# Retention operands issued behind bank copies, alternating token halves in three channel tiles, and the last token tile's residual added inside its PSUM bank

## The chip, the core and the metric

The kernel runs on one core of one Trainium2 chip. Its time is the device time of one execution in microseconds (us). A core has four engines that matter here, each with its own program that it works through in order: TensorE (PE) multiplies, with its weight loads as a second stream (PEld); VectorE (DVE) and ScalarE (ACT) do elementwise work; SyncE (SP) issues transfers (DMA) between memory and the on-chip buffer, and ACT can issue some too. Engines wait for each other by semaphores. Products of TensorE land in PSUM, which has eight banks of 512 fp32 columns on 128 partitions, and DVE or ACT read them from there.

## The reference

The kernel computes one layer on 512 tokens of width 1024, with 16 learned meta tokens put in front:

```python
u = rms_norm(x) @ w_in                 # eight groups: rnn values and gates, q, k, v, retention gates, two mixing gates
rnn: causal conv of 4 taps, sigmoid gates a and x, a linear scan over the tokens, GELU gate
ret: 4 heads, chunked retention with decay, head_rms, then * silu(gate)
mix = sigmoid(..) * (rnn @ w_branch_rnn) + sigmoid(..) * (ret @ w_branch_ret)
h = x + mix @ w_out
f = rms_norm(h) @ w_up                 # 6144 columns, causal conv of 3 taps, gelu(half) * other half
out = rms_norm(h + f @ w_down) * norm_final_g
```

Input and output are fp32.

## The kernel before

**fp32 as two fp16 parts.** Each operand is split into a high fp16 part and a low one. `split` (L92 to L96) is one ACT copy that writes the high part (L94) and one DVE SCALAR_TENSOR_TENSOR that writes the remainder (L95). A product is then three matmuls, high by high, high by low and low by high, in the order of `SPLIT = ((0,0),(0,1),(1,0))`, where the first index is that of the weights. A weight is loaded by a DMA into a tile `raw` (three buffers) and split into a tile `wt`. Of the trace's names, `xh` and `xl` are the two parts of the normalised input, `xs` those of an intermediate.

**Start.** The first ten channel tiles of `w_in` are the values of the recurrent branch (loop at L686, `n` from 0 to 9). `conv_product(n)` (L632) multiplies 1024 input rows by 128 channels for all tokens, which stand in two halves `HR` of 266 and 265 columns, each in a PSUM bank of its own. The tiles 0 to 2 were begun earlier with one half each (`early`), and do the other half here. The tiles from 3 on go through `project` (L428): all 24 matmuls of one half, then the 24 of the other. A weight tile covers half of the 1024 rows, so a channel reads two of them. Between two channels stand the 12 gate matmuls of the channel three before (`rnn_gates`, L654, on `xs` and `gw`). `conv_taps` (L642) reads the product from PSUM, once on ACT (L644) and three times on DVE (L646), and only then is its pair of banks free; there are four pairs, shared with the gates, so that a channel's product waits for the taps of the channel two before it.

**Mixing.** After retention, the kernel runs the gates and the two branches' products. `fast_products` (L872) is a form of Strassen's algorithm with seven products, which share the banks `pa`, `pb` and `pe`. Where a bank is used on by the next product, its content is first put aside by an ACT copy, `keep` (L887), into `kept` or `last`; this copy has high priority and is remembered in `last_keep[0]`. The product T1, for one, can't start in `pa` until `kept` is copied from it. The gated retention outputs `or` are turned into operands `ob` of such a product by `ob_forms`: `differences` (four DVE operations, L1082 to L1085), `plain` and `formed` (five splits, each on ACT and on DVE). They stand in the list `pending`, and `flush` (L1108) takes one of them at each step of the mixing (`advance`). The order of each engine's program follows from a scheduler that looks at priorities and at what an instruction has been told to stand behind (`tc.issue_after`). `behind_copy()` tells it to stand behind the last bank copy, but only while `gating[0]` is true; at L1161 that is set to False, and so `flush` in the mixing puts its step in without any such rule.

**End.** The output is made for four token tiles of 128 rows. `down_plain` (L1602) multiplies the last weight unit into a bank, 12 matmuls of 512 columns. Then, per token tile in the order 2, 3, 0, 1: DVE adds the residual (`hu`, L1702), ACT squares and sums (L1704, with its ACTIVATION_READ_ACCUMULATOR), DVE multiplies by the final weight (L1705), ACT takes the root (L1707), DVE the reciprocal (L1709), and then DVE scales 512 of the columns (L1710) and ACT the other 512 (L1712); two transfers of 128 rows by 2 KB write them out (L1711 on SP, L1713 on SP too, or, for the last tile, on ACT's queue). The last token tile is tile 1, in the bank P7. The first half of each row was multiplied by the final weight earlier (`weigh`, L1673).

Of the kernel before, what the change touches and what calls it, by code (L numbers as in the profile page):

```python
# [8 lines left out]
F32 = mybir.dt.float32  # L9
F16 = mybir.dt.float16  # L10
AF = mybir.ActivationFunctionType
ORDERED = {mybir.EngineType.PE, mybir.EngineType.Activation, mybir.EngineType.DVE}
ALU = mybir.AluOpType

P = 128
# [4 lines left out]
KD = D // P  # L20
# [33 lines left out]
def hybrid_block_kernel(ctx, tc, x, meta, norm_mix_g, w_in, conv_w, conv_b, rg_a_w, rg_a_b,  # L54
                        rg_x_w, rg_x_b, lam, w_brnn, w_bret, w_out, norm_ffn_g, w_up,
                        fconv_w, fconv_b, w_down, norm_final_g, rope_t, decay_t, out):
    nc = tc.nc
# [5 lines left out]
    work = ctx.enter_context(tc.tile_pool(name="work", bufs=8))  # L63
    small = ctx.enter_context(tc.tile_pool(name="small", bufs=4))
# [11 lines left out]
    def acc(name):  # L76
        return psum["acc"].tile([P, 2, 512], F32, name=name, tag="acc")
# [6 lines left out]
    def xslot(shape, dtype, name):  # L84
        return xp.tile(shape, dtype, name=name, tag="x")

    def piece(shape, dtype, name):
        return pieces.tile(shape, dtype, name=name, tag="s")
# [20 lines left out]
    def kmaj(w, k0, nk, c0, ncol):  # L109
        return w[k0 * P:(k0 + nk) * P, c0:c0 + ncol].rearrange("(k p) c -> p k c", p=P)  # L110
# [3 lines left out]
    def unit(nk, ncol, parts, fast=False):  # L114
        units.append((nk, ncol, parts, fast))
        return len(units) - 1
# [3 lines left out]
    for i in range(5):  # L120
        u = unit(8, 256, [(0, 0, kmaj(w_in, 0, 8, o_ur + 256 * i, 256))])
# [71 lines left out]
    def unit_load(cuts=1):  # L193

        nk, ncol, parts, fast = units[len(loaded)]
        raw = wraw.tile([P, 2048], F32, name="raw")
        n = nk * ncol
        rv = raw[:, :n].rearrange("p (k c) -> p k c", k=nk)
        for k0, c0, ap in parts:
            load(rv[:, k0:k0 + ap.shape[1], c0:c0 + ap.shape[2]], ap)  # L200
        loaded.append(len(loaded))
        if fast:
            return fast_steps(rv, nk // 2, ncol // 2)
        hk = nk // 2
        hn = hk * ncol
        tiles = []

        def step(i, c):
            def run():
                if c == 0:  # L210
                    tiles.append(wsp.tile([P, 2, 1024], F16, name="wt"))
                sl = slice(c * hn // cuts, (c + 1) * hn // cuts)
                split(tiles[i][:, 0, sl], tiles[i][:, 1, sl], raw[:, i * hn:(i + 1) * hn][:, sl], SW)
            return run

        wviews.append(lambda a, k, c0, m: tiles[k // hk][:, a, k % hk * ncol + c0:k % hk * ncol + c0 + m])
        return [step(i, c) for i in range(2) for c in range(cuts)]
# [66 lines left out]
    last_keep = [None]  # L284
    gating = [True]

    def behind_copy():

        return tc.issue_after(last_keep[0]) if gating[0] and last_keep[0] else nullcontext()
# [8 lines left out]
    def emit_step():  # L298
        u, run = steps[done[0]]
        while len(loaded) < min(u + 3, len(units)):  # L300
            queue(unit_load())
        run()
        done[0] += 1

    def queue(new):
        steps.extend((len(loaded) - 1, run) for run in new)

    def get(u):
        current[0] = max(current[0], u)
        while len(loaded) <= u:  # L310
            queue(unit_load())
        while done[0] < len(steps) and steps[done[0]][0] <= u:
            emit_step()
        return wviews[u]
# [96 lines left out]
    SPLIT = ((0, 0), (0, 1), (1, 0))  # L411

    def x_of(hi, lo):
        tv = (hi, lo)
        return lambda a, k, c0, n: tv[a][:, k, c0:c0 + n]

    xf = x_of(xh, xl)

    def half_of(ps, halves, hf):
        c0, n = (512 - halves[0][1], halves[0][1]) if hf == 0 else (0, halves[1][1])  # L420
        return ps[:, hf, c0:c0 + n]
# [3 lines left out]
        n = n or halves[0][1] + halves[1][1]  # L425
        return ps.rearrange("p a b -> p (a b)")[:, c0:c0 + n]

    def project(ps, w, col, src, halves, nk):  # L428

        for hf, (c0, n) in enumerate(halves):  # L430
            for k in range(nk):
                for aw, ax in SPLIT:
                    nc.tensor.matmul(half_of(ps, halves, hf), w(aw, k, col, P), src(ax, k, c0, n),  # L433
                                     start=k == 0 and (aw, ax) == (0, 0), stop=k == nk - 1 and aw == 1)

# [2 lines left out]
    HR = [(0, 266), (266, 265)]  # L438
# [4 lines left out]
    def project_half(ps, w, col, src, halves, hf):  # L443
        c0, n = halves[hf]
        for k in range(KD):
            for aw, ax in SPLIT:
                mm = nc.tensor.matmul(half_of(ps, halves, hf), w(aw, k, col, P), src(ax, k, c0, n),  # L447
                                      start=k == 0 and (aw, ax) == (0, 0), stop=k == KD - 1 and aw == 1)
        return mm.ins
# [182 lines left out]
    def conv_product(n):  # L632
        u, col = u_ur[n]
        if n in early:
            ps = early.pop(n)
            project_half(ps, get(u), col, xf, HR, 1)
        else:
            ps = acc("ps")
            project(ps, get(u), col, xf, HR, KD)
        return ps  # L640

    def conv_taps(n, ps):  # L642
# [43 lines left out]
    for n in range(NR):  # L686
        ps = conv_product(n)
# [41 lines left out]
    for n in range(NR):  # L729
        ps = acc("ps")  # L730
        u, col = u_ug[n // 2], (n % 2) * P
# [45 lines left out]
    for h in range(HEADS):  # L777
        t = [[piece([P, 2, T], F16, f"qk{h}{i}{m}") for m in range(2)] for i in range(2)]
# [329 lines left out]
    def flush(n=1):  # L1108

        for _ in range(min(n, len(pending))):  # L1110
            with behind_copy():
                pending.pop(0)()

    def advance(run, *names):
# [83 lines left out]
    def branch(us, src, nk):  # L1198
        ps = acc("pm")
        project(ps, get(us.pop(0)), 0, src, HH, nk)  # L1200
        tick(2)
        return run_of(ps, HH)
# [20 lines left out]
    for i in range(2):  # L1223
# [5 lines left out]
        ps = branch(u_ba, oa_of, NR)  # L1229
# [6 lines left out]
        gate_a(i + 1, after)  # L1236
    mix_first(5, branch(u_ba, oa_of, NR))
    flush(len(pending))

    def gate_b(i):  # L1240
# [23 lines left out]
    h2 = [h2p[i // 2][:, i % 2] for i in range(4)]  # L1264
# [137 lines left out]
    halves = slice(0, 256), slice(256, 512)  # L1402
# [181 lines left out]
    gfin = xslot([P, D], F32, "gfin")  # L1584
# [3 lines left out]
    o2 = out.rearrange("o t d -> (o t) d")  # L1588
    inv_d = 1.0 / D
    un = 1.0 / (SW * S_ACT)  # L1590
    sums = small.tile([P, 4, 4], F32, name="sums", bufs=1)
# [7 lines left out]
                                 start=q % 6 == 0 and tt == 0 and i == 0 and (ax, aw) == (0, 0),  # L1599
                                 stop=q % 6 == last and i == 1 and ax == 1, skip_group_check=True)  # L1600

    def down_plain(pc, tt):  # L1602

        w = wviews[u_dn[11]]
        n = 0
        for half in range(2):
            for b in range(2):
                t, c0 = acts[10 + b]["A%d%d" % (tt // 2 + 1, half + 1)]
                for ax, aw in SPLIT:
                    nc.tensor.matmul(pc, t[:, ax, c0 + tt % 2 * P:c0 + tt % 2 * P + P], w(aw, 2 * half + b, 0, 512),  # L1610
                                     start=n == 0, stop=n == 11)
                    n += 1

    def square(tt, cols, n):
# [42 lines left out]
    pd = products()  # L1657
# [9 lines left out]
    for tt in range(4):  # L1667
        junk = work.tile([P, 512], F32, name="junk", tag="w")
        nc.scalar.activation(junk.rearrange("p (a b) -> p a b", a=2),
                             h2[tt].rearrange("p (a b) -> p a b", a=2)[:, :, 0:256],  # L1670
                             AF.Square, accum_out=sums[:, tt, 0:1])

    def weigh(tt, c0):  # L1673
        v = h2[tt].rearrange("p (a b) -> p a b", a=2)[:, :, c0:c0 + 256]
        nc.vector.tensor_tensor(v, v, gfin.rearrange("p (a b) -> p a b", a=2)[:, :, c0:c0 + 256], op=ALU.mult)

    for tt in range(4):
        weigh(tt, 0)
        nc.vector.tensor_scalar(sums[:, tt, 1:2], sums[:, tt, 0:1], inv_d, EPS, op0=ALU.mult, op1=ALU.add)


    pd = products()
# [10 lines left out]
                next(run)  # L1693
    nc.scalar.activation(sq_t, sums[:, 3, 1:2], AF.Sqrt)
    for nm, tt in (("spare", 2), ("P1", 3), ("P6", 0), ("P7", 1)):
        down_plain(pd[nm], tt)
        pv = pd[nm].rearrange("p (a b) -> p a b", a=2)
        hv = h2[tt].rearrange("p (a b) -> p a b", a=2)[:, :, 256:512]
        gv = gfin.rearrange("p (a b) -> p a b", a=2)[:, :, 256:512]
        hu = work.tile([P, 512], F32, name="hu", tag="w")  # L1700
        huv = hu.rearrange("p (a b) -> p a b", a=2)
        nc.vector.scalar_tensor_tensor(huv, pv, un, hv, op0=ALU.mult, op1=ALU.add)  # L1702
        junk = work.tile([P, 512], F32, name="junk", tag="w")
        nc.scalar.activation(junk, hu, AF.Square, accum_out=sums[:, tt, 2:3])  # L1704
        nc.vector.tensor_tensor(hv, huv, gv, op=ALU.mult)  # L1705
        sd = small.tile([P, 1], F32, name="sd")
        nc.scalar.activation(sd, sums[:, tt, 2:3], AF.Sqrt, scale=inv_d, bias=sums[:, tt, 1:2])  # L1707
        rs = small.tile([P, 1], F32, name="rs")
        nc.vector.reciprocal(rs, sd)  # L1709
        nc.vector.tensor_scalar_mul(h2[tt][:, 0:512], h2[tt][:, 0:512], rs)  # L1710
        nc.sync.dma_start(o2[tt * P:(tt + 1) * P, 0:512], h2[tt][:, 0:512])  # L1711
        nc.scalar.activation(h2[tt][:, 512:1024], h2[tt][:, 512:1024], AF.Copy, scale=rs)  # L1712
        (nc.scalar if tt == 1 else nc.sync).dma_start(o2[tt * P:(tt + 1) * P, 512:1024], h2[tt][:, 512:1024])  # L1713
    psum["scope"].close()


# [45 lines left out]
```

## Time and profile before

| what | value |
|---|---|
| time, median of 3 runs | 1061.51 us (1061.37 to 1062.74) |
| profiled execution, its own time | 1061.5 us |
| span of that execution in the profile | 1059.8 us, so 1.7 us lie outside |
| granted TensorE clock | 0.999 of full speed |
| TensorE busy | 1039.7 us, 98% of the span |
| VectorE busy | 872.8 us, 82% |
| ScalarE busy | 594.0 us, 56% |

A row of the profile's timeline has the start in us from the start of the span, the duration in us, the engine, the line of the kernel, the operation, and what is written from what. `x12` stands for twelve like instructions drawn together, whose duration runs from the first's start to the last's end. The brackets at the end, such as `[0.83 <-DVE wt L95]`, give the time that the engine stood idle ahead of this row and what released it. Matmuls are pipelined: one of 266 columns is on record for 0.28 us, while the next one starts some 0.11 us after it. On DVE and ACT too, a row is some 0.1 us longer than the distance to the next one's start, where the next is ready.

### The profile page before, as it was taken

The numbers are of one execution on the slowest core, as the hardware profiler recorded it, in microseconds if no ns is written. First come the engines' busy times: TensorE is split into PE (matmuls) and PEld (weight loads), VectorE is DVE, ScalarE is ACT, GpSimd is POOL, SyncE is SP. The second block draws the span as 40 slices with busy tenths as digits, with TensorE's granted clock in tenths as the row PEclk, the third lists the DMA queues.
The fourth block names the chain that finished last, engine by engine and source line by source line (L and its number), as shares of the span: only waits on it lengthen the run. The fifth ranks groups of instructions, "written<-read, shape, count | busy, mean of one in ns | idle before, by whom it ended". The sixth has DMA issues, their size and how long they took to land.

```text
span 1059.8 us, 21437 instructions
## 1 busy us (share of the span) xinstructions
PE 1039.7 (98%) x9187; PEld 865.9 (82%) x9187; DVE 872.8 (82%) x1328; ACT 594.0 (56%) x941; POOL 6.9 (1%) x20
## 2 busy tenths in 40 slices
PE   9999999999999999999999999999999999999997
PEld 6888887875588888888888886588888888888885
DVE  6885699988669999996787885479989898988975
ACT  7568973434356768665454453375555455554442
POOL 2000000000000000000000000000000000000000
PEclk9999999999999999999999999999999999999999
DMA  9231243431012132344334356032423324214312
GB/s 295 97 127 58 81 140 120 159 123 40 1 41 93 68 105 66 107 114 128 108 113 129 98 219 194 1 116 85 160 87 113 120 81 136 65 61 139 101 41 80
DMA packets 109056, 111.52 MB, mean 105 GB/s; under 512 B 5675, under 2 KB 100625, under 8 KB 108961
## 3 DMA queue, kind: packets, MB, share of 16 engines
q1 hardware_dynamic: 108512, 109.74, 32.5%
q8 instruction: 72, 1.18, 0.5%
q10 hardware_dynamic: 160, 0.27, 0.1%
q0 software_dynamic: 288, 0.14, 0.1%
q14 instruction: 24, 0.19, 0.1%
HBM read 108.04 MB, written 2.10 MB: 104 GB/s over the span
## 4 chain that ended last, share of the span: by engine, by line
PE 72%; DVE 16%; ACT 9%; issue 2%; DMA 0%; ACTq 0%; DVEq 0%
PE ps L433 25%; PE P L1598 10%; PE pa L881 9%; DVE wt L95 5%; PE ps L1315 4%; PE pe L881 4%; PE pm L433 4%; PE ps L945 4%; ACT wt L94 2%; PE pb L881 2%; PE pa L1485 2%; PE ps L1035 2%; PE ps L447 2%; DVE rnn L680 1%; PE pa L969 1%
## 5 line engine op out<-in xcount | busy, mean ns | idle before, releaser
L433 PEld LDWEIGHTS <-wt 128*128 128x128 f16 x3840 | 372.5, 97 | 56.0 <-DVE t L770 2.6
L95 DVE SCALAR_TENSOR_TENSOR wt<-raw,wt 128x1024 f16<-128x1024 f32 (+2 forms) x286 | 310.0, 1100 | 57.1 <-ACT wt L94 56.2
L94 ACT ACTIVATE wt<-raw 128x1024 f16<-128x1024 f32 (+2 forms) x286 | 268.2, 958 | 118.7 <-PE P L1598 25.6
L881 PEld LDWEIGHTS <-wt 128*128 128x128 f16 x2016 | 195.2, 97 | 33.5 <-issue 6.7
L433 PE MATMUL ps<-x2h,wt 128*128 128x258 f16 (+1 forms) x1184 | 196.2, 272 | 0.0
L433 PE MATMUL ps<-xh,wt 128*128 128x258 f16 (+4 forms) x1056 | 179.0, 274 | 3.7 <-DVE t L770 2.9
L433 PE MATMUL ps<-x2l,wt 128*128 128x256 f16 (+1 forms) x592 | 160.9, 272 | 0.0
L433 PE MATMUL ps<-xl,wt 128*128 128x256 f16 (+4 forms) x528 | 144.5, 274 | 0.0
L1598 PE MATMUL P<-wt,act 128*128 128x256 f16 x792 | 88.3, 273 | 0.0
L1598 PEld LDWEIGHTS <-act 128*128 128x128 f16 x792 | 77.5, 98 | 9.0
L881 PE MATMUL pa<-xs,wt 128*128 128x258 f16 x576 | 71.3, 273 | 3.0 <-ACT kept L887 2.6
L1463 DVE SCALAR_TENSOR_TENSOR cv<-ps,vt,cv 128x512 f32<-128x512 f32 x80 | 59.3, 745 | 9.1 <-ACT cv L1461 8.5
L433 PE MATMUL pm<-oa,wt 128*128 128x256 f16 (+1 forms) x480 | 54.1, 273 | 0.0
L262 DVE TENSOR_TENSOR raw<-raw 128x1024 f32<-128x1024 f32 x43 | 52.4, 1219 | 0.7
L881 PE MATMUL pa<-ob,wt 128*128 128x257 f16 x384 | 45.7, 274 | 0.6 <-ACT last L887 0.5
L1315 PE MATMUL ps<-wt,mx 128*128 128x512 f16 x192 | 44.3, 378 | 0.0
L945 PE MATMUL ps<-wt,xh 128*128 128x512 f16 x128 | 38.3, 379 | 0.6 <-ACT qk L94 0.5
L1461 ACT ACTIVATE cv<-ps,vt,vt 128x512 f32<-128x512 f32 x40 | 30.5, 766 | 11.9 <-PE ps L433 11.9
L1485 PEld LDWEIGHTS <-wt 128*128 128x128 f16 x336 | 32.6, 97 | 4.4
L94 ACT ACTIVATE qk<-t 128x514 f16<-128x514 f32 (+1 forms) x16 | 10.2, 638 | 40.9 <-DVE t L772 40.9
L1315 PEld LDWEIGHTS <-mx 128*128 128x128 f16 x192 | 17.6, 98 | 18.5
L447 PEld LDWEIGHTS <-wt 128*128 128x128 f16 x288 | 27.9, 97 | 5.0 <-issue 0.6
(319 smaller groups left out, 1503.3 us busy)
## 6 DMA issues: line engine op xcount, KB each, us to landing
raw<-in_w_in SPq DMA_DIRECT2D x36, 1024.0 KB, 5.0
raw<-in_w_up SPq DMA_DIRECT2D x24, 1024.0 KB, 5.2
raw<-in_w_down SPq DMA_DIRECT2D x48, 256.0 KB, 3.4
raw<-in_w_branch_ret SPq DMA_DIRECT2D x16, 512.0 KB, 4.8
raw<-in_w_in SPq DMA_DIRECT2D x12, 512.0 KB, 4.6
raw<-in_w_branch_rnn SPq DMA_DIRECT2D x8, 640.0 KB, 4.7
raw<-in_w_out SPq DMA_DIRECT2D x4, 1024.0 KB, 5.0
xin<-in_x SPq DMA_DIRECT2D x4, 512.0 KB, 5.6
```

The lines of the kernel that those rows point to most:

```text
L94: a = nc.scalar.activation(hi, src, AF.Copy, scale=s)
L95: b = nc.vector.scalar_tensor_tensor(lo, src, s, hi, op0=ALU.mult, op1=ALU.subtract)
L262: nc.vector.tensor_tensor(pair, pair, rv[:, :, right].rearrange("p (h k) c -> p h k c", h=2), op=ALU.add)
L433: nc.tensor.matmul(half_of(ps, halves, hf), w(aw, k, col, P), src(ax, k, c0, n), start=k == 0 and (aw, ax) == (0, 0), stop=k == nk - 1 and ...
L447: mm = nc.tensor.matmul(half_of(ps, halves, hf), w(aw, k, col, P), src(ax, k, c0, n), start=k == 0 and (aw, ax) == (0, 0), stop=k == KD - ...
L881: nc.tensor.matmul(ps[:, :n], ws[k // 4](wf, aw, k % 4), src(xf_, ax, k), start=first and k == 0 and (aw, ax) == (0, 0), stop=k == last_k ...
L945: nc.tensor.matmul(pb, xf(ax, k, XF + j0, nb), w(aw, k % 4, 0, 512), start=i == 0, stop=i == 23)
L1315: nc.tensor.matmul(ps[:, n], mx[k][:, a, c0:c0 + P], wo[k // 2](aw, k % 2, n * 512, 512), start=k == 0 and (a, aw) == (0, 0), stop=k == ks ...
L1461: nc.scalar.activation(vv_, taps[2], AF.Identity, scale=vt2[:, 96 + ch:97 + ch], bias=bias)
L1463: nc.vector.scalar_tensor_tensor(vv_, taps[j], vt2[:, 48 * j + ch:48 * j + ch + 1], vv_, op0=ALU.mult, op1=ALU.add)
L1485: nc.tensor.matmul(ps[:, :258], w(wf, aw, k), x2_form(xf_, ax, k), start=first and k == 0 and (aw, ax) == (0, 0), stop=k == 3 and aw == 1, ...
L1598: nc.tensor.matmul(pd[:, 256 * tt:256 * tt + 256], t[:, ax, c0 + tt * P:c0 + tt * P + P], w(wf, aw, i), start=q % 6 == 0 and tt == 0 and i ...
```

## The change

There are three edits. First, `flush` puts each pending step behind the last bank copy in all cases, not only while `gating[0]` is true. Second, `project` gets a flag `turns`: with it the loop over the halves is the innermost, so that successive matmuls go to the two banks in turn; `conv_product` sets it for n < 6, which, as the tiles 0 to 2 take the other branch, is for the tiles 3, 4 and 5. Third, for the last token tile (`LAST = 1`) an ACT copy puts the residual, divided by the scale of the products, into the bank P7 ahead of the matmuls, and these add to it. ACT then squares straight from the bank, with the scale in its operand and an epsilon term scaled in advance (`sums[:, LAST, 3]`, a new small DVE operation), and one DVE SCALAR_TENSOR_TENSOR makes the output's half out of the bank, the reciprocal and the final weight. The two transfers each carry 256 runs of 1 KB in place of 128 of 2 KB. `weigh` becomes a SCALAR_TENSOR_TENSOR of the same size. Lines behind `project` stand one later in the changed kernel, those of the end more.

```diff
-    def project(ps, w, col, src, halves, nk):
+    def project(ps, w, col, src, halves, nk, turns=False):
-        for hf, (c0, n) in enumerate(halves):
-            for k in range(nk):
-                for aw, ax in SPLIT:
+        both = [0, 1]
+        for hfs in [both] if turns else [[0], [1]]:
+            for k, (aw, ax), hf in [(k, s, hf) for k in range(nk) for s in SPLIT for hf in hfs]:
+                    c0, n = halves[hf]
                     nc.tensor.matmul(half_of(ps, halves, hf), w(aw, k, col, P), src(ax, k, c0, n),
...
-            project(ps, get(u), col, xf, HR, KD)
+            project(ps, get(u), col, xf, HR, KD, n < 6)
...
         for _ in range(min(n, len(pending))):
-            with behind_copy():
+            with tc.issue_after(last_keep[0]):
                 pending.pop(0)()
...
+    nc.vector.tensor_scalar_mul(sums[:, LAST, 3:4], sums[:, LAST, 1:2], 1.0 / (un * un))
...
+        if tt == LAST:
+            nc.scalar.activation(pv, hv, AF.Copy, scale=1.0 / un)
+            down_plain(pd[nm], tt, True)
+            junk = work.tile([P, 512], F32, name="junk", tag="w")
+            nc.scalar.activation(junk, pd[nm], AF.Square, scale=un, accum_out=sums[:, tt, 2:3])
+            nc.scalar.activation(sd, sums[:, tt, 2:3], AF.Sqrt, scale=inv_d / (un * un), bias=sums[:, tt, 3:4])
+            nc.vector.reciprocal(rs, sd)
+            ob_ = o2[tt * P:(tt + 1) * P].rearrange("t (a b) -> t a b", a=2)
+            nc.vector.scalar_tensor_tensor(hv, pv, rs, gv, op0=ALU.mult, op1=ALU.mult)
+            nc.sync.dma_start(ob_[:, :, 256:512], hv)
+            nc.scalar.activation(hb[:, :, 0:256], hb[:, :, 0:256], AF.Copy, scale=rs)
+            nc.scalar.dma_start(ob_[:, :, 0:256], hb[:, :, 0:256])
+            break
```

TensorE, the product of a channel tile that goes through `project` (tile 4): the name `ps` is its pair of banks, and the number of columns tells the half, 266 for the first and 265 for the second. Before:

```order
L433 MATMUL ps<-xh,wt 128x266
L433 LDWEIGHTS wt
L433 MATMUL ps<-xl,wt 128x266
L433 LDWEIGHTS wt
L433 MATMUL ps<-xh,wt 128x266
L433 LDWEIGHTS wt
L433 MATMUL ps<-xh,wt 128x266
```

After:

```order
L434 MATMUL ps<-xh,wt 128x266
L434 LDWEIGHTS wt
L434 MATMUL ps<-xh,wt 128x265
L434 LDWEIGHTS wt
L434 MATMUL ps<-xl,wt 128x266
L434 LDWEIGHTS wt
L434 MATMUL ps<-xl,wt 128x265
```

The same 48 matmuls and weight loads are there, but the second half now goes along with the first, so that each part of the weights is asked for at half the pace.

ScalarE in the mixing, around 452 to 461 us of the span: `g` are the gates, `kept` is the bank copy on which T1 waits, `ob` the retention operands. Before:

```order
L920 ACT_TABLE_LOAD
L920 ACTIVATE g_5557<-g_5557 128x257
L887 ACTIVATE kept<-pa 128x257
L920 ACTIVATE g_5557<-pa 128x257
L94 ACTIVATE wt<-raw 128x1024
L920 ACTIVATE g_5556<-g_5556 128x514
L94 ACTIVATE ob_5835<-or_5016 128x257
L887 ACTIVATE kept<-pa 128x257
L94 ACTIVATE ob<-or_5017 128x514
```

After:

```order
L888 ACTIVATE kept<-pa 128x257
L921 ACT_TABLE_LOAD
L921 ACTIVATE g_5557<-g_5557 128x257
L921 ACTIVATE g_5557<-pa 128x257
L94 ACTIVATE wt<-raw 128x1024
L921 ACTIVATE g_5556<-g_5556 128x514
L888 ACTIVATE kept<-pa 128x257
L94 ACTIVATE ob_5835<-or_5016 128x257
L94 ACTIVATE ob<-or_5017 128x514
```

The second copy `kept` now stands ahead of the operand `ob_5835`, and directly behind the gate `g_5556`; the first one stands ahead of the gate's table load.

VectorE at the same place, 450 to 455 us: the sum `g_5557<-pe,last` (L908 before, L909 after) is the one that frees the bank `pe` for the product T4. Before:

```order
L95 SCALAR_TENSOR_TENSOR wt<-raw,wt 128x1024 x2
L95 SCALAR_TENSOR_TENSOR wt<-raw,wt 128x640 x2
L1206 SCALAR_TENSOR_TENSOR m<-pm,g_5346 128x514
L95 SCALAR_TENSOR_TENSOR ob<-or_4354,ob 128x514
L904 TENSOR_TENSOR g_5556<-pb,kept 128x257
L95 SCALAR_TENSOR_TENSOR ob<-y,ob 128x514
L95 SCALAR_TENSOR_TENSOR ob<-d,ob 128x514
L908 TENSOR_TENSOR g_5557<-pe,last 128x257
L95 SCALAR_TENSOR_TENSOR wt<-raw,wt 128x512
```

After:

```order
L95 SCALAR_TENSOR_TENSOR ob_5440<-or_4353,ob_5440 128x257
L95 SCALAR_TENSOR_TENSOR wt<-raw,wt 128x1024 x2
L95 SCALAR_TENSOR_TENSOR wt<-raw,wt 128x640
L1207 SCALAR_TENSOR_TENSOR m<-pm,g_5346 128x514
L95 SCALAR_TENSOR_TENSOR wt<-raw,wt 128x640
L905 TENSOR_TENSOR g_5556<-pb,kept 128x257
L95 SCALAR_TENSOR_TENSOR ob<-or_4354,ob 128x514
L95 SCALAR_TENSOR_TENSOR wt<-raw,wt 128x512
L1124 TENSOR_TENSOR or_5018<-or_5018,rt 128x514
L909 TENSOR_TENSOR g_5557<-pe,last 128x257
L95 SCALAR_TENSOR_TENSOR ob<-y,ob 128x514
L95 SCALAR_TENSOR_TENSOR ob<-d,ob 128x514
```

The two operands `ob<-y` and `ob<-d` now stand behind that sum; a weight part of 512 columns, the scaling `or_5018` (L1123 before) and the 257-column part of `ob_5440` have come ahead of it.

More of the change, by code (lines that the diff above doesn't have):

```diff
@@ L1600, in down_product, with down_plain @@
                                  stop=q % 6 == last and i == 1 and ax == 1, skip_group_check=True)
-    def down_plain(pc, tt):
+    def down_plain(pc, tt, seeded):
         w = wviews[u_dn[11]]
@@ L1610, in down_plain @@
                     nc.tensor.matmul(pc, t[:, ax, c0 + tt % 2 * P:c0 + tt % 2 * P + P], w(aw, 2 * half + b, 0, 512),
-                                     start=n == 0, stop=n == 11)
+                                     start=n == 0 and not seeded, stop=n == 11, skip_group_check=seeded)
                     n += 1
@@ L1671, in hybrid_block_kernel @@
                              AF.Square, accum_out=sums[:, tt, 0:1])
+    LAST = 1
     def weigh(tt, c0):
         v = h2[tt].rearrange("p (a b) -> p a b", a=2)[:, :, c0:c0 + 256]
-        nc.vector.tensor_tensor(v, v, gfin.rearrange("p (a b) -> p a b", a=2)[:, :, c0:c0 + 256], op=ALU.mult)
+        nc.vector.scalar_tensor_tensor(v, v, 1.0 / un if tt == LAST else 1.0,
+                                       gfin.rearrange("p (a b) -> p a b", a=2)[:, :, c0:c0 + 256],
+                                       op0=ALU.mult, op1=ALU.mult)
     for tt in range(4):
@@ L1695, in hybrid_block_kernel @@
     for nm, tt in (("spare", 2), ("P1", 3), ("P6", 0), ("P7", 1)):
-        down_plain(pd[nm], tt)
         pv = pd[nm].rearrange("p (a b) -> p a b", a=2)
-        hv = h2[tt].rearrange("p (a b) -> p a b", a=2)[:, :, 256:512]
-        gv = gfin.rearrange("p (a b) -> p a b", a=2)[:, :, 256:512]
+        hb = h2[tt].rearrange("p (a b) -> p a b", a=2)
+        hv, gv = hb[:, :, 256:512], gfin.rearrange("p (a b) -> p a b", a=2)[:, :, 256:512]
+        sd = small.tile([P, 1], F32, name="sd")
+        rs = small.tile([P, 1], F32, name="rs")
+        if tt == LAST:
[11 more added lines that the diff above has]
+            break
+        down_plain(pd[nm], tt, False)
         hu = work.tile([P, 512], F32, name="hu", tag="w")
@@ L1705, in hybrid_block_kernel @@
         nc.vector.tensor_tensor(hv, huv, gv, op=ALU.mult)
-        sd = small.tile([P, 1], F32, name="sd")
         nc.scalar.activation(sd, sums[:, tt, 2:3], AF.Sqrt, scale=inv_d, bias=sums[:, tt, 1:2])
-        rs = small.tile([P, 1], F32, name="rs")
         nc.vector.reciprocal(rs, sd)
@@ L1712, in hybrid_block_kernel @@
         nc.scalar.activation(h2[tt][:, 512:1024], h2[tt][:, 512:1024], AF.Copy, scale=rs)
-        (nc.scalar if tt == 1 else nc.sync).dma_start(o2[tt * P:(tt + 1) * P, 512:1024], h2[tt][:, 512:1024])
+        nc.sync.dma_start(o2[tt * P:(tt + 1) * P, 512:1024], h2[tt][:, 512:1024])
     psum["scope"].close()
```

## The prediction

> **What bounds the kernel now.** I read the page first: busy times and the chain that ended last.
>
> ```profile
> span 1059.8 us, 21437 instructions
> PE 1039.7 (98%) x9187; PEld 865.9 (82%) x9187; DVE 872.8 (82%) x1328; ACT 594.0 (56%) x941; POOL 6.9 (1%) x20
> PE 72%; DVE 16%; ACT 9%; issue 2%; DMA 0%; ACTq 0%; DVEq 0%
> ```
>
> TensorE is busy for 98% and makes 72% of the chain. None of the edits takes a matmul away, so the only thing to win is TensorE's idle time, 1059.8 − 1039.7 = 20.1 us of the span, and the work behind its last matmul. I therefore went through TensorE's timeline for the rows with a wait in brackets, then through ACT's and DVE's rows just ahead of each of them. The edits touch idle time at three places.
>
> **Part 1, alternating halves.** TensorE's rows at the start, first tile 4 and the gates behind it, then the first matmul of tile 5, then tile 9, which doesn't stall:
>
> ```profile
> 39.90 0.28 PE L433 MATMUL ps<-xh,wt 128*128 128x266 f16 x1
> ...
> 42.65 0.40 PE L433 MATMUL ps<-xh,wt 128*128 128x266 f16 x2 [0.83 <-DVE wt L95]
> ...
> 46.53 0.84 PE L433 MATMUL ps<-xs,gw 128*128 128x264 f16 x6
> ...
> 47.88 0.28 PE L433 MATMUL ps<-xh,wt 128*128 128x266 f16 x1
> ...
> 75.14 0.28 PE L433 MATMUL ps<-xh,wt 128*128 128x266 f16 x1
> ...
> 80.60 1.51 PE L433 MATMUL ps<-xs,gw 128*128 128x264 f16 x12
> ```
>
> and DVE's rows there, the low parts of tile 4's two weight tiles and the taps of tile 3:
>
> ```profile
> 39.00 1.22 DVE L95 SCALAR_TENSOR_TENSOR wt<-raw,wt 128x1024 f16<-128x1024 f32 x1
> ...
> 41.37 1.22 DVE L95 SCALAR_TENSOR_TENSOR wt<-raw,wt 128x1024 f16<-128x1024 f32 x1
> ...
> 44.03 2.37 DVE L646 SCALAR_TENSOR_TENSOR rnn<-ps,cwr,rnn 128x528 f32<-128x528 f32 x3
> ```
>
> Without a stall the 48 matmuls of a channel take 80.60 − 75.14 = 5.46 us, 0.114 each. Tile 4 took 46.53 − 39.90 = 6.63: it lost 1.17, as its weights' low parts were ready only at 40.22 and 42.59. With the halves in turn the first low part is wanted by the fifth matmul, at 39.90 + 4 × 0.114 = 40.36, and the second by the 29th, at 43.09. Both are there by then, so tile 4 ends at 45.36, **1.17 earlier**. Neither ACT nor DVE waits for TensorE here, so the splits don't move. What is late next is the pair of banks. Tile 5 waits for taps that end at 44.03 + 2.37 = 46.40 and would arrive at 47.88 − 1.17 = 46.71, with 0.31 to spare; the tiles behind it stand to their taps in the same way, each a little tighter or looser. Tiles 3 and 5 have no stall, and for them the order costs nothing, if changing the bank is free (a rival below).
>
> Does the gain reach the end? ACT's first wait for TensorE after that, a later wait of ACT for a transfer, and TensorE's wait at 162.75:
>
> ```profile
> 81.48 0.70 ACT L662 ACTIVATE rnn<-ps,vt 128x528 f32<-128x528 f32 x1 [1.51 <-PE ps L433]
> ```
>
> ```profile
> 153.20 2.00 ACT L94 ACTIVATE wt<-raw 128x1024 f16<-128x1024 f32 x2 [5.48 <-DMA raw<-in_w_in]
> ```
>
> ```profile
> 162.75 0.28 PE L433 MATMUL ps<-xh,wt 128*128 128x256 f16 x1 [2.30 <-DVE t L770]
> ```
>
> At 81.48 ACT waits for TensorE and had been free since 79.97, so the chain of the recurrent branch, which DVE and ACT carry from there to 162.75, starts 1.17 earlier (with 1.51 of room). The transfer awaited at 153.20 is issued when an earlier `raw` is free, that is by the same chain, so I let it move along. Bounds of the term: 0, if banks or transfers hold it, and −1.17; I take **−1.17**, as each of these waits has room in its row.
>
> **Part 2, operands behind the bank copies.** The stalls of TensorE at the beginning of the mixing:
>
> ```profile
> 425.06 1.48 PE L881 MATMUL pa<-xs,wt 128*128 128x258 f16 x12 [0.28 <-ACT kept L887]
> ...
> 439.61 1.48 PE L881 MATMUL pa<-xs,wt 128*128 128x258 f16 x12 [0.33 <-ACT kept L887]
> ```
>
> ```profile
> 453.66 0.27 PE L881 MATMUL pe<-xh,wt 128*128 128x258 f16 x1 [0.70 <-DVE g L908]
> ...
> 458.84 0.27 PE L881 MATMUL pb<-xh,wt 128*128 128x258 f16 x1
> 460.53 1.48 PE L881 MATMUL pa<-xs,wt 128*128 128x258 f16 x12 [1.42 <-ACT kept L887]
> ```
>
> ACT and DVE there:
>
> ```profile
> 438.65 0.63 ACT L920 ACTIVATE g<-g 128x514 f32<-128x514 f32 x1 [1.84 <-DVE g L915]
> ```
>
> ```profile
> 457.47 0.62 ACT L920 ACTIVATE g<-g 128x514 f32<-128x514 f32 x1
> 459.79 0.42 ACT L94 ACTIVATE ob<-or 128x257 f16<-128x257 f32 x1 [1.70 <-DVE or L1067]
> 460.11 0.37 ACT L887 ACTIVATE kept<-pa 128x257 f32<-128x257 f32 x1
> ```
>
> ```profile
> 452.59 0.68 DVE L95 SCALAR_TENSOR_TENSOR ob<-d,ob 128x514 f16<-128x514 f32 x1
> 453.19 0.41 DVE L908 TENSOR_TENSOR g<-pe,last 128x257 f32<-128x257 f32 x1
> 453.53 1.81 DVE L95 SCALAR_TENSOR_TENSOR wt<-raw,wt 128x512 f16<-128x512 f32 x2
> ...
> 457.00 0.41 DVE L915 TENSOR_TENSOR g<-pe,kept 128x257 f32<-128x257 f32 x1
> ```
>
> At 425.06 the copy comes free of the forms ahead of it and up to 0.28 goes. But at 439.61 the copy stands behind the gate of 438.65, which waits for a DVE sum that the edit doesn't move; TensorE, early, waits there for the longer, and what was won is given back: 0 for these two together.
>
> At 453.66 it gets worse. Ahead of the sum L908 there go two forms of 514 columns (0.60 each to the next start), and there come a weight part of 512 (0.60), a scaling of 514 (0.60) and a form of 257 (0.34): + 1.54 − 1.20 = +0.34, and T4 starts at 454.00.
>
> At 460.53 it gets better. In the trace, `kept` stands behind the form of 459.79, which waited 1.70 for DVE's `or`. In the new order it stands right behind the gate of 457.47. That gate waits for L915, at 457.00 before; it now has the 0.34, and two forms (1.20) ahead of it, less the weight part of 512 that has gone ahead (0.60): 457.94, so the gate is at 457.94 + 0.47 = 458.41, the copy, 0.52 behind it, at 458.93 and done at 459.30, and T1 starts at 459.35. TensorE itself comes from the product before at 458.84 + 0.11 + 0.34 = 459.29. So T1 starts 460.53 − 459.35 = 1.18 earlier, the 0.34 included. The form that had held the copy now waits alone; TensorE doesn't need it for long. Further on, ACT waits for TensorE:
>
> ```profile
> 480.22 0.74 ACT L94 ACTIVATE wt<-raw 128x640 f16<-128x640 f32 x1 [4.12 <-PE pm L433]
> ```
>
> There the engines take their time from TensorE again, and the gain stays. The new orders differ no more after about 500 us, so I leave later stalls as they are. Bounds: −2.73, if all four stalls went (0.28 + 0.33 + 0.70 + 1.42), and +0.34, if only the loss came true. I take **−1.18**, my count through the queues.
>
> **Part 3, the end.** The last matmuls, then DVE, ACT, and the transfers' issues:
>
> ```profile
> 1052.05 1.46 PE L1610 MATMUL P<-wt,act 128*128 128x512 f16 x6
> ```
>
> ```profile
> 1053.67 0.68 DVE L1702 SCALAR_TENSOR_TENSOR hu<-P,h 128x512 f32<-128x512 f32 x1
> ...
> 1055.67 0.49 DVE L1710 TENSOR_SCALAR h<-h,rs 128x512 f32<-128x512 f32 x1
> ```
>
> ```profile
> 1047.80 0.63 ACT L1704 ACTIVATE junk<-hu 128x512 f32<-128x512 f32 x1 [11.90 <-DVE hu L1702]
> ...
> 1053.27 0.72 ACT L1712 ACTIVATE h<-h,rs 128x512 f32<-128x512 f32 x1 [0.23 <-DVE rs L1709]
> 1054.39 0.63 ACT L1704 ACTIVATE junk<-hu 128x512 f32<-128x512 f32 x1 [0.40 <-DVE hu L1702]
> ...
> 1056.42 0.38 ACTq L1713 DMA_DIRECT2D out<-h  x1
> ```
>
> ```profile
> 1056.19 0.33 SPq L1711 DMA_DIRECT2D out<-h  x1
> ```
>
> The product ends at 1053.51. Before, DVE's sum (1053.67) and then the square (1054.39) follow. Now the square reads the bank, but ACT is at L1712 of the token tile before until about 1053.27 + 0.62 = 1053.89: the square starts 0.50 earlier, not 0.7. From the square on the chain has the same members up to the reciprocal, so ACT's transfer is issued 0.50 earlier, at 1055.92. On DVE an operation like that of 1053.67 (0.68) takes the place of one of 0.49, so SP's transfer goes out 0.50 − 0.19 = 0.31 earlier, at 1055.88. The two are then issued together instead of 0.23 apart, and with twice the runs; if the second queues behind the first for that 0.23, the end gains 0.27. The seeding copy lies in ACT's idle stretch of 11.90 us ahead of 1047.80, at the price of a copy of 512 columns, 0.7, without cover. `weigh` changes its operation and not its size; with the new small DVE operation it stands behind TensorE work: nothing. Bounds: 0 (the runs of 1 KB eat all of it) and −0.50; I take **−0.3**.
>
> The Trainium skill ("DMA: Bandwidth & Descriptors", in "Anatomy of one DMA", on where the 2 us go) says that most of a transfer's fixed time is the wait until the last byte is confirmed. By it the end would follow the issue, −0.50, and the sum be 0.2 lower; the trace has no pair of transfers issued together at the end to show which.
>
> **Sum.** −1.17 − 1.18 − 0.3 = −2.65. The profiled execution took 1061.5 us, the median to within 0.01: 1061.5 − 2.65 = **1058.9 us**, a span of about 1057.2.
>
> **Rivals.** *The start's gain is lost.* Were the transfer awaited at 153.20 set by the queue and not by free buffers, the recurrent chain would stand where it stood and 1.17 be gone: 1060.0. For it: 5.48 us of waiting. Against: the wait is for a buffer's turn and no stretch near it moves much.
>
> *The mixing's gain is lost.* DVE is the tighter queue there. If the gate of 457.47 is later by another 0.9, the copy behind it is no better off than before, only the start and the end remain, and TensorE may carry the 0.34: 1061.5 − 1.17 − 0.3 + 0 to 0.34 = 1060.0 to 1060.4. For it: one hand count through some forty instructions.
>
> *All mixing stalls go:* 1061.5 − 1.17 − 2.73 − 0.3 = 1057.3.
>
> *Slower: a change of bank costs TensorE time.* The three tiles have 144 matmuls, nearly each now in another bank than the one before. At 18 ns each (2.65 / 144) nothing is left, and at 33 ns (4.77 / 144) it is slower by over 2.12; if each waited out the one before, 0.28 in place of 0.114, it would be 144 × 0.166 = 24 us, 1083. Against it, a group whose bank changes with every third matmul, and one that stays in its bank:
>
> ```profile
> 646.25 5.13 PE L1315 MATMUL ps<-wt,mx 128*128 128x512 f16 x23
> ```
>
> ```profile
> 1042.96 2.78 PE L1610 MATMUL P<-wt,a 128*128 128x512 f16 x12
> ```
>
> The first takes (5.13 − 0.38) / 22 = 0.216 each, the second (2.78 − 0.38) / 11 = 0.218: no cost per change. Bounds: 0, and about 6 ns if 0.002 of each matmul escaped me, 0.9 in all; I take 0. For it there is only that no row shows a change at every matmul.
>
> **How the numbers follow.** A measurement here can tell 0.2%, 2.12 us, from no change: faster means below 1059.4. Chances: forecast 0.52; all mixing stalls gone 0.08; start lost 0.14; mixing lost 0.17; both lost (about 1061.2) 0.03; slower by bank changes 0.06. Faster 0.60, same 0.34, slower 0.06. The range, 1057.5 to 1060.9, reaches from short of the case of all mixing stalls to past both single losses, and leaves out that case's lower half, both lost and slower, about 0.13.
>
> **What would show it.** Right: the row of 42.65 has no wait, tile 4's 48 matmuls take 5.5 us, ACT's wait of 1.51 at 81.5 falls to about 0.3, and TensorE at 162.75 is 1.2 earlier. In the mixing, a wait of about 1.0 for L909 and a wait of under 0.2 for the copy ahead of T1. At the end, a square some 0.5 us behind the last matmul and issues of both transfers within 0.1 us. Wrong: matmuls further apart than 0.114 in the tiles 3 to 5; TensorE no earlier at 195 us; a new wait for the retention operands `ob` around 461 to 480.

## The result, and the profile after

| what | before | changed |
|---|---|---|
| median of 22 runs | 1062.26 us (1061.30 to 1062.76) | 1060.02 us (21 from 1059.52 to 1060.69, one of 2199.91) |
| ratio of the two, without the run of 2199.91 | | 0.9982, 95% interval 0.9976 to 0.9989 |
| profiled execution | 1061.5 us | 1060.05 us |
| its span | 1059.8 us | 1058.3 us |

The change is 1.9 us faster (0.0018 of 1062.26), its interval 1.2 to 2.5 us. The forecast was 2.65 us, or 0.25%: the sign is right, the size is some 0.7 of the forecast. By the line that the prediction drew, faster below 1059.4 us, a median of 1060.02 doesn't count as faster, though the interval of the ratio lies below 1.

In part of the executions of each kernel here, of before too, TensorE runs at half clock for some 3 us behind its idle time at 162 us, and the whole is about 0.8 us longer (shown in the last section), so times told as "without the half clock" are medians over the quicker of the two groups into which the times fall: 1061.5 us for before and 1059.88 for the changed kernel, a gain of 1.6 us.

The page of the changed kernel: its chain has moved from DVE and ACT to TensorE by four points (72% before).

```profile
span 1058.3 us, 21434 instructions
PE 1040.1 (98%) x9187; PEld 866.7 (82%) x9187; DVE 872.2 (82%) x1327; ACT 594.4 (56%) x942; POOL 6.9 (1%) x20
...
PE 76%; DVE 15%; ACT 8%; issue 1%; ACTq 0%; DVEq 0%
```

The start, TensorE's timeline: the first two matmuls of tile 4, now one of each half, the gates behind it, the first two matmuls of tile 5, the gates behind that, and the old stall at 162.75.

```profile
40.16 0.39 PE L434 MATMUL ps<-xh,wt 128*128 128x266 f16 x2
...
45.69 1.51 PE L434 MATMUL ps<-xs,gw 128*128 128x264 f16 x12
47.04 0.39 PE L434 MATMUL ps<-xh,wt 128*128 128x266 f16 x2
...
52.57 1.51 PE L434 MATMUL ps<-xs,gw 128*128 128x264 f16 x12
...
161.99 0.28 PE L434 MATMUL ps<-xh,wt 128*128 128x256 f16 x1 [2.32 <-DVE t L771]
```

Tile 4 takes 45.69 − 40.16 = 5.53 us in place of 6.63, and no row of it has a wait. Tile 5, which had no stall before, takes 52.57 − 47.04 = 5.53 too. At 161.99 TensorE is 0.76 earlier than before on this clock. But this execution's first channel matmul also came later, at 13.94 for 13.68; counted from there the start won 0.76 + 0.26 = 1.02 us.

The mixing, TensorE with T1's first matmuls as the last row, then ACT, then DVE:

```profile
439.00 1.48 PE L882 MATMUL pa<-xs,wt 128*128 128x258 f16 x12 [0.98 <-ACT kept L888]
...
453.38 0.27 PE L882 MATMUL pe<-xh,wt 128*128 128x258 f16 x1 [1.03 <-DVE g L909]
...
458.74 1.48 PE L882 MATMUL pa<-xs,wt 128*128 128x258 f16 x12
```

```profile
457.80 0.62 ACT L921 ACTIVATE g<-g 128x514 f32<-128x514 f32 x1
458.32 0.36 ACT L888 ACTIVATE kept<-pa 128x257 f32<-128x257 f32 x1
460.12 0.94 ACT L94 ACTIVATE ob<-or 128x257 f16<-128x257 f32 x2 [1.43 <-DVE or L1068]
```

```profile
457.32 0.42 DVE L916 TENSOR_TENSOR g<-pe,kept 128x257 f32<-128x257 f32 x1
```

The wait of 1.42 ahead of T1 is gone, the copy stands right behind the gate, and the retention operand behind it now does the waiting (1.43). Ahead of T4 the wait is 1.03 in place of 0.70. The waits at 425.06 and 439.61 (0.28 and 0.33) have become one of 0.98. T1 starts 460.53 − 458.74 = 1.79 earlier than before, of which 0.76 had come from the start: the mixing gave 1.03.

The end, the last matmuls, ACT's square out of the bank, and the two transfers:

```profile
1050.28 1.46 PE L1611 MATMUL P<-wt,act 128*128 128x512 f16 x6
```

```profile
1051.50 0.72 ACT L1731 ACTIVATE h<-h,rs 128x512 f32<-128x512 f32 x1 [0.23 <-DVE rs L1728]
1052.13 0.58 ACT L1711 ACTIVATE junk<-P 128x512 f32<-128x512 f32 x1
...
1054.11 0.64 ACTq L1718 DMA_DIRECT2D out<-h  x1
```

```profile
1054.14 0.64 SPq L1716 DMA_DIRECT2D out<-h  x1
```

TensorE ends 1.77 earlier than before (1052.05 to 1050.28). Against its last matmul the square is 0.49 earlier, SP's issue 0.28 and ACT's 0.54. Yet the span is only 1.5 shorter: 0.27 us of the gain has been lost behind the issues. Issuing a transfer takes 0.64 us, for 0.33 and 0.38 before. The view of the DMA issues, last stretch of the span, has the time from issue to landing as its last number, before and after:

```profile
out<-h SPq DMA_DIRECT2D x1, 256.0 KB, 2.0
out<-h ACTq DMA_DIRECT2D x1, 256.0 KB, 2.5
```

```profile
out<-h ACTq DMA_DIRECT2D x1, 256.0 KB, 2.6
out<-h SPq DMA_DIRECT2D x1, 256.0 KB, 3.3
```

That time counts from the start of the issue. The last landing was at 1056.42 + 2.5 = 1058.9; now it is SP's, 1054.14 + 3.3 = 1057.4: 1.5 earlier, as the span.

### The profile page after: what moved, and what is told of

It is laid out like the page before. It is cut to its first block, busy times and chain, and to the rows that moved or that the text cites. A ratio compares the mean times of both kernels' runs of the same rounds, so it can differ in the third digit from the quotient of the medians.

```text
span 1058.3 us, 21434 instructions
## 1 busy us (share of the span) xinstructions
PE 1040.1 (98%) x9187; PEld 866.7 (82%) x9187; DVE 872.2 (82%) x1327; ACT 594.4 (56%) x942; POOL 6.9 (1%) x20
## 3 DMA queue, kind: packets, MB, share of 16 engines
q8 instruction: 72, 1.18, 0.5%
## 4 chain that ended last, share of the span: by engine, by line
PE 76%; DVE 15%; ACT 8%; issue 1%; ACTq 0%; DVEq 0%
PE ps L434 26%; PE P L1599 10%; PE pa L882 9%; DVE wt L95 4%; PE pe L882 4%; PE ps L1316 4%; PE ps L946 4%; PE pm L434 3%; PE ps L448 3%; PE pb L882 2%; PE pa L1486 2%; ACT wt L94 2%; PE ps L1036 2%; PE pa L970 1%; DVE rnn L681 1%
## 5 line engine op out<-in xcount | busy, mean ns | idle before, releaser
L434 PE MATMUL ps<-xl,wt 128*128 128x256 f16 (+4 forms) x528 | 140.8, 274 | 0.0
```

## The experiments

The theory: the start and the mixing each win 1.0 us on their own, and the end loses some 0.3 to 0.4, because its transfers have twice the runs. Its rivals are that one gain is the other's passed on, that the end's loss is due to both transfers being issued at once, and that a change of bank costs TensorE time. All kernels, without the half clock, against before on the same chip:

| kernel | us | against before | ratio of all runs, 95% interval |
|---|---|---|---|
| halves in turn alone | 1060.44 | −1.02 | 0.9990 (0.9982 to 0.9999) |
| steps behind copies alone | 1060.44 | −1.02 | 0.9992 (0.9983 to 1.0001) |
| new end alone | 1061.86 | +0.40 | 1.0001 (0.9992 to 1.0010) |
| changed, without the new end | 1059.61 | −1.96 | 0.9979 (0.9970 to 0.9988) |
| changed, runs of 2 KB | 1059.25 | −2.21 | 0.9975 (0.9966 to 0.9984) |
| halves in turn in tile 4 alone | 1060.49 | −1.05 | 0.9992 (0.9983 to 1.0001) |
| halves in turn in tiles 3 to 9 | 1060.93 | −0.61 | 0.9993 (0.9984 to 1.0002) |
| one step behind its copy | 1059.87 | −1.67 | 0.9983 (0.9974 to 0.9991) |
| in turn, one step, runs of 2 KB | 1058.74 | −2.80 | 0.9977 (0.9968 to 0.9986) |
| the same, in turn in tile 4 alone | 1058.70 | −2.87 | 0.9970 (0.9958 to 0.9982) |

Before is 1061.46 to 1061.57 in these comparisons, as medians of 7 to 15 executions. Each time is a median of 3 to 9 executions that lie within 0.6 us. The rows come from three chips, so where two of them are compared, their differences against before are the safer figures, and these too are good to about 0.1. The intervals on the right are over all runs and so contain the half clock's share too; for the versions whose gain is 1.05 or less, and for the new end alone, they contain 1 or come close to it, so the readings below rest on the times without the half clock together with the rows of the traces.

### Each part alone

The new `project` with `n < 6` in before:

```diff
-            project(ps, get(u), col, xf, HR, KD)
+            project(ps, get(u), col, xf, HR, KD, n < 6)
```

> Before with the alternating halves in the tiles 3 to 5 alone. Theory (the start is won for good, the banks cost nothing): 1.0 to 1.1 us faster than before, tile 4's 48 matmuls in 5.5 us with no wait in them, and TensorE's wait at about 162 us some 1.05 us earlier, counted from the first channel matmul. Rival (the 0.27 us by which the changed kernel's first channel matmul is later, 13.94 for 13.68, belongs to the edit): 0.75 faster. Rival (a change of bank costs time): the tiles 3 and 5 take more than 5.46 us.

Measured −1.02. Tile 4's rows:

```profile
39.84 0.39 PE L434 MATMUL ps<-xh,wt 128*128 128x266 f16 x2
...
45.37 0.50 PE L434 MATMUL ps<-xs,gw 128*128 128x264 f16 x3
```

Again 5.53 us. In this execution the first channel matmul is at 13.60, so the 0.26 by which it was later in the changed kernel doesn't belong to the edit. TensorE's stall at 162 us:

```profile
161.68 0.28 PE L434 MATMUL ps<-xh,wt 128*128 128x256 f16 x1 [2.34 <-DVE t L771]
```

Counted from the first channel matmul it is 148.08, for 162.75 − 13.68 = 149.07 in before: 0.99 earlier. The gain is the start's own. The second rival is right in kind: tile 5 takes 52.24 − 46.71 = 5.53 here for 5.46 before.

The new `flush` in before:

```diff
-            with behind_copy():
+            with tc.issue_after(last_keep[0]):
```

> Before with the pending steps behind the bank copies alone. Theory: 1.0 to 1.2 us faster; the wait ahead of T1 at 460.5 us goes, the one for the sum ahead of T4 at 453.7 grows from 0.70 to about 1.0, and the waits at 425 and 439.6 sum to what they were. Rival (the mixing's gain in the changed kernel was the start's, passed on): no change.

Measured −1.02: the mixing's gain is its own as well. TensorE's waits are those of the changed kernel:

```profile
440.40 1.48 PE L881 MATMUL pa<-xs,wt 128*128 128x258 f16 x12 [0.98 <-ACT kept L887]
...
454.78 0.27 PE L881 MATMUL pe<-xh,wt 128*128 128x258 f16 x1 [1.03 <-DVE g L908]
...
460.14 1.48 PE L881 MATMUL pa<-xs,wt 128*128 128x258 f16 x12
```

The wait ahead of T1 is gone and the one ahead of T4 has grown, as expected. One point failed: the waits at 425 and 439.6 don't sum to what they were, 0.28 + 0.33, but have become one of 0.98.

The new end in before, with the lines of the change's last block, `weigh` and `down_plain`:

```diff
+        if tt == LAST:
+            nc.scalar.activation(pv, hv, AF.Copy, scale=1.0 / un)
+            down_plain(pd[nm], tt, True)
...
+            nc.sync.dma_start(ob_[:, :, 256:512], hv)
```

> Before with the last token tile's new end alone. Theory (the square starts 0.5 us earlier, but the two transfers of 256 runs of 1 KB, issued together, land 1.0 to 1.3 us later after their issue): 0.2 to 0.4 us slower than before; both issues about 0.3 and 0.5 us earlier against the last matmul, SP's transfer landing 3.3 us after its issue in place of 2.0. Rival (the prediction's term): 0.3 us faster.

Measured +0.40 without the half clock; the interval over all runs contains 1, so by it alone no loss is shown. Here ACT's transfer is the late one, not SP's:

```profile
out<-h ACTq DMA_DIRECT2D x1, 256.0 KB, 3.3
out<-h SPq DMA_DIRECT2D x1, 256.0 KB, 2.5
```

The prediction's term of −0.3 falls. Which of the two lands late differs, but in both kernels one of them takes 3.3 us. Counted from the start of the last matmuls' row, the last landing comes some 0.3 us later than before in both.

The changed kernel with the end of before:

> The changed kernel without its new end: alternating halves and all pending steps behind the bank copies, the end as before. Theory (the parts add up, and the new end with runs of 1 KB costs 0.4): 1.9 to 2.1 us faster than before, so 0.3 to 0.5 faster than the changed kernel. Rival (the new end gains in company with the other parts): no faster than the changed kernel.

It is the kernel with the first two edits above and nothing else. Measured −1.96, for −1.6 of the changed kernel: some 0.35 faster, within the expected 0.3 to 0.5. The times themselves, 1059.61 and 1059.88, lie 0.27 apart, but they were taken in different comparisons. The parts add up: −1.02 − 1.02 is −2.04 for −1.96, and with + 0.40 it is −1.64 for the changed kernel's −1.6.

### What the end costs

```diff
-            nc.sync.dma_start(ob_[:, :, 256:512], hv)
             nc.scalar.activation(hb[:, :, 0:256], hb[:, :, 0:256], AF.Copy, scale=rs)
-            nc.scalar.dma_start(ob_[:, :, 0:256], hb[:, :, 0:256])
+            nc.sync.dma_start(o2[tt * P:(tt + 1) * P, 0:512], h2[tt][:, 0:512])
+            nc.scalar.dma_start(o2[tt * P:(tt + 1) * P, 512:1024], h2[tt][:, 512:1024])
```

> The changed kernel, but its last two transfers carry 128 runs of 2 KB each, as before, and so each waits for both DVE and ACT. Theory (the number of runs costs the time at the end): 0.6 to 0.9 us faster than the changed kernel, 2.3 to 2.8 us faster than before, with landings 2.0 to 2.6 us after the issue. Rival (it is that both are issued at once and share the engines, whatever the runs): as the changed kernel, SP's landing still about 3.3 us.

Measured −2.21, which is some 0.6 faster than the changed kernel, as expected, and a little under the expected 2.3 to 2.8 against before. SP's issue and ACT's, and the landings:

```profile
1053.76 0.33 SPq L1717 DMA_DIRECT2D out<-h  x1
```

```profile
1053.78 0.39 ACTq L1718 DMA_DIRECT2D out<-h  x1
```

```profile
out<-h SPq DMA_DIRECT2D x1, 256.0 KB, 2.3
out<-h ACTq DMA_DIRECT2D x1, 256.0 KB, 2.7
```

Both are still issued together, 0.02 apart, so being issued at once costs 0.2 to 0.3 against the 2.0 and 2.5 of before, and the doubled runs cost the rest: a last landing of 3.3 in place of 2.7, in which an issue of 0.64 in place of 0.33 to 0.39 is contained. The rival falls, but for these 0.2 to 0.3. The two other versions with runs of 2 KB, further down, have landings of 2.3 and 2.7 as well. With 2 KB the new end does gain, 2.21 − 1.96 = 0.25. The traces agree: from the start of the last matmuls' row (1049.86 here) to the last landing it is 6.6 us, for 6.9 in before and 7.2 in the changed kernel.

### What the alternation costs

```diff
-            project(ps, get(u), col, xf, HR, KD)
+            project(ps, get(u), col, xf, HR, KD, n == 4)
```

> Before with the alternating halves in tile 4 alone. Theory (only tile 4's late low weight parts are passed by): the same gain as with the tiles 3 to 5, 0.9 to 1.1 us faster than before. Rival (the gain needs the tiles 3 or 5 too, as their weights are late as well): less than 0.6.

Measured −1.05: tile 4 alone carries the whole gain. Then the same with `True` in place of `n == 4`:

> Before with the alternating halves in all seven channel tiles that go through project (3 to 9), 336 matmuls in place of 144. Theory (a change of bank is free): the matmuls stay 0.114 us apart and the time is that with the tiles 3 to 5, 0.9 to 1.1 us faster than before. Rival (a change costs 6 ns, the bound given before): 1.2 us lost again over the 192 further ones, no faster than before.

Measured −0.61. Neither forecast holds: taking turns isn't free, and it doesn't cost 6 ns for each change of bank either. A tile that doesn't stall, tile 9, here:

```profile
74.05 0.39 PE L434 MATMUL ps<-xh,wt 128*128 128x266 f16 x2
...
79.58 0.50 PE L434 MATMUL ps<-xs,gw 128*128 128x264 f16 x3
```

It takes 5.53 us for the 5.46 of before: 0.07 more, or 1.4 ns per matmul. With the bank, the half of the input that is read changes at each matmul too; no run parts the two. Over the four tiles more than with `n < 6` that is 0.28 of the 0.41 that this version is slower; the rest lies within what medians of four and five executions can tell.

### Where the mixing's gain sits

One pending step alone behind its copy, the plain forms of the last head's first half:

```diff
+        plain.first = (h, i) == (3, 0)
         return [differences, plain, formed]
...
-            with behind_copy():
+            with tc.issue_after(last_keep[0]) if getattr(pending[0], "first", False) else behind_copy():
```

> Before with a single pending step put behind the bank copy, the plain forms of the last head's first half, so that only the copy ahead of T1 at 460.5 us and the form of 459.8 change places on ACT; DVE's order is that of before. Theory (the gain is that the copy no longer stands behind a form that waits for DVE): 1.4 to 1.6 us faster, more than with all steps, as the waits at 439.6 and 453.7 stay as they are. Rival (the gain comes from the other forms' moving behind DVE's sums): no change.

Measured −1.67, more than all steps together and slightly more than expected. On ACT the copy and the form have changed places, and TensorE goes on without a wait:

```profile
457.77 0.62 ACT L920 ACTIVATE g<-g 128x514 f32<-128x514 f32 x1
458.29 0.37 ACT L887 ACTIVATE kept<-pa 128x257 f32<-128x257 f32 x1
460.09 0.94 ACT L94 ACTIVATE ob<-or 128x257 f16<-128x257 f32 x2 [1.43 <-DVE or L1067]
```

```profile
439.90 1.48 PE L881 MATMUL pa<-xs,wt 128*128 128x258 f16 x12 [0.32 <-ACT kept L887]
...
453.96 0.27 PE L881 MATMUL pe<-xh,wt 128*128 128x258 f16 x1 [0.70 <-DVE g L908]
...
459.14 0.27 PE L881 MATMUL pb<-xh,wt 128*128 128x258 f16 x1
459.25 1.48 PE L881 MATMUL pa<-xs,wt 128*128 128x258 f16 x12
```

That one swap is the gain. That it is more than the wait of 1.42 in before's row comes from how idle time is counted, from the recorded end of the matmul ahead, 0.27 long: the starts were 460.53 − 458.84 = 1.69 apart and are 0.11 here, 1.58 less. The other steps' moves cost about 0.65 of it (1.67 − 1.02): here the waits at 439 and ahead of T4 are those of before, 0.32 and 0.70.

### The parts put together

The halves in turn, that one step, and the end with runs of 2 KB:

> The start's alternating halves, that single step behind the copy in place of all steps, and the new end with runs of 2 KB. Theory (the terms add up: 1.0, 1.5 and 0.2): 2.6 to 2.8 us faster than before, 0.8 to 1.1 faster than the changed kernel. Rival (with the start won, the mixing is bound by DVE and the single step's advantage goes): about 2.2 faster, as the changed kernel with runs of 2 KB.

Measured −2.80: the terms add up to within 0.14 (−1.02 − 1.67 − 0.25 = −2.94), and it is some 1.1 to 1.2 faster than the changed kernel. With `n == 4` in place of `n < 6`:

> As the version with the halves in turn, the single step and runs of 2 KB, but with the halves in turn in tile 4 alone. Theory (each tile in turn costs 0.065 us and only tile 4 has something to win): 0.05 to 0.15 us faster than that version, 2.8 to 3.0 faster than before. Rival (the order of the tiles 3 and 5 matters elsewhere): no faster than that version.

Measured −2.87, by 0.04 us the lowest time of all. The expected 0.05 to 0.15 is too small for three executions of each to settle; for it speak only the rows of 5.53 in tiles that had no stall. This version beats both kernels: 1058.70 for 1061.57 and 1059.88.

## Why the prediction was right, point by point

The sign is right, and the measured 1060.02 us lies in the range of 1057.5 to 1060.9. That alone proves little: 1060.0 is also what the prediction gave for the loss of the start's gain, and for the loss of the mixing's. It is the parts, each measured alone, that bear out the mechanism of the first two and refute the third. Forecast was faster, with a chance of 0.60; by its own line of 1059.4 the change is the same, which had 0.34. All three terms came out worse than forecast, so no error made up for another.

**What bounds.** Right: TensorE is busy for 1040 us in both, and what was gained came out of its idle time at the start and in the mixing.

**Part 1, forecast −1.17, measured −1.02.** The mechanism is right: no wait in tile 4, the banks in time, the gain carried past the transfer wait at 153 and on to the end. Mis-sized is the cost of taking turns, which the sum put down to the changing bank and took as 0 between bounds of 0 and 6 ns: it is 1.4 ns per matmul, 0.07 us in each of the tiles 4 and 5, which is nearly all of the missing 0.15. The sign of being wrong that the prediction named, matmuls further apart than 0.114 in the tiles 3 to 5, did show, at 0.115; the other two, TensorE no earlier at 195 us and a new wait for `ob` around 461 to 480, did not. One detail failed: ACT's wait at 81.5 fell to 0.77, not 0.3. ACT had waited for TensorE a little earlier too, and so came some 0.3 earlier itself. ACT's rows of before at tile 7:

```profile
66.77 1.04 ACT L94 ACTIVATE wt<-raw 128x1024 f16<-128x1024 f32 x1
67.85 0.70 ACT L662 ACTIVATE rnn<-ps,vt 128x528 f32<-128x528 f32 x1
68.58 0.70 ACT L662 ACTIVATE gi<-ps,vt 128x528 f32<-128x528 f32 x1
```

The starts are 1.08 and 0.73 apart; with the halves in turn alone they are 0.94 and 0.59, 0.28 less in all.

**Part 2, forecast −1.18, measured −1.02.** The count through the queues held. T4's wait grew by 0.33 for a forecast 0.34, and from T4 to T1 the gain was 1.79 − 0.28 = 1.51 for a forecast 1.18 + 0.34 = 1.52. Mis-sized is the pair at 425 and 439: it was put at 0 and cost 0.16. In the changed kernel the copy at 438.58 is only 0.61 earlier than before where the start had brought 0.76; the splits on DVE ahead of its sum began that much later. Which moved instruction does that was not tried alone. Two figures beside the count were off. For the copy to be no better off than before, the gate would have to come later by 1.18, not by the rival's 0.9; and the bound of −2.73 takes T1's stall as 1.42, where the starts of the single step's kernel show 1.58.

**Part 3, forecast −0.3, measured +0.40 alone, some +0.3 in the changed kernel.** This step failed. All up to the issue came as worked out: the square 0.49 earlier (0.50), the issues 0.28 and 0.54 earlier (0.31 and 0.50), together within 0.03 us, and the seeding copy hidden. Wrong was the price put on the transfers: "if the second queues behind the first for that 0.23, the end gains 0.27". The doubled runs make the last landing 0.6 us later, 0.3 of it in a longer issue. The lower bound of the term was 0, and that it could be a loss was left out.

**The rivals.** "The start's gain is lost" and "The mixing's gain is lost" fall with the two parts measured alone. "All mixing stalls go" did not come. "Slower: a change of bank costs TensorE time" was right in kind and far too small to decide. The Trainium skill's rule ("DMA: Bandwidth & Descriptors", in "Anatomy of one DMA", on transfers that GpSimd issues), that most of the fixed time is the wait for the last byte's receipt, would have had the end follow the issue. The landings of 2.0 to 3.3 us for the same 256 KB, on the queues of SP and ACT, show that here the number of runs matters as well.

## What to carry to other kernels

Look for the copy that frees a bank standing behind an operand that waits for another engine, and move that one step: moving its neighbours with it cost over a third of the gain here (0.65 of 1.67 us). Taking two halves in turn halves the pace at which weights are wanted; it pays in the one tile whose weights are late, and costs a little in each other. At the very end of a kernel, keep the output's runs long, since a transfer's issue and its landing are both on the path.

## What the runs showed of the hardware

TensorE's clock after an idle time of 2.3 us. The view of windows over 163 to 165 us, whose columns are the stretch, its length, the busy time of TensorE, its weight loads, DVE, ACT and POOL with their counts, the granted clock, the DMA share and GB/s, for before and for the kernel with the new end alone:

```profile
163.00:165.00 2.00, 2.00 (x21) 1.77 (x19) 2.00 (x4) 0.47 (x1) 0.00 (x0) 1.00 0.03 8
```

```profile
163.00:165.00 2.00, 2.00 (x11) 1.39 (x10) 2.00 (x5) 0.54 (x1) 0.00 (x0) 0.50 0.04 8
```

In the second the granted clock is 0.50 and 11 matmuls go through where there were 21. That kernel's TensorE timeline from the idle time on, with the lines where the distance of two starts is 0.21 us and where it is 0.11 again:

```profile
162.68 0.40 PE L433 MATMUL ps<-xh,wt 128*128 128x256 f16 x1 [2.30 <-DVE t L770]
162.87 0.42 PE L433 MATMUL ps<-xl,wt 128*128 128x256 f16 x1
163.08 0.63 PE L433 MATMUL ps<-xh,wt 128*128 128x256 f16 x2
...
166.05 0.27 PE L433 MATMUL ps<-xl,wt 128*128 128x256 f16 x1
166.16 0.38 PE L433 MATMUL ps<-xh,wt 128*128 128x256 f16 x2
```

The half clock lasts from 162.68 to about 166.0, 3.3 us. In the kernel with tile 4 alone in turn both of its ends lie among matmuls: they start 0.11 apart again from 161.58 on, behind an idle time of 2.33 us, then 0.21 apart from about 162.1 to 165.5, which is 3.4 us. TensorE's wait at 195 us, 0.61 in before, is gone in both of these executions; what it doesn't absorb makes the execution some 0.7 to 0.9 us longer. Of the twelve profiled executions, before's and the changed kernel's among them, six have a granted clock of 0.50 to 0.59 in this stretch and six have 1.00. It is no kernel's property: by their times 8 of the changed kernel's 21 runs have it, and 12 of 22 of before. The Trainium skill ("TensorE: Matmul & The Clock Gate", in "Part 1: The HAM clock gate") tells of a free-running window of about 3.4 us, with half rate after an idle window and full rate after a busy one. The 3.3 to 3.4 us of half clock agree with the window, and that only part of the executions have it agrees with its running free; but the idle time is 2.3 us, so less than a whole window of it can be enough. That a version without the idle time would be rid of it wasn't tried.

Two halves taken in turn, so that the bank and the half of the input change with every matmul, cost 1.4 ns per matmul of 265 or 266 columns, 1.2% of the 0.114 us between two starts. And 256 KB out in 256 runs of 1 KB took 0.64 to 0.67 us to issue, in 128 runs of 2 KB 0.33 to 0.39.
